# A decoder block on one core: the opening in fixed orders, four PSUM tiles for its transposes, and the first chunk's output in another slot

## The chip, the cores and the metric

The kernel runs on one core of one Trainium2 chip. The metric is the time on the device in microseconds, from the first to the last instruction and what lies around them; less is better.

## The reference

One layer of a hybrid block over 1024 positions of 1024 channels, in fp32:

```
h = LN(x)
xs, z, B, C, dt, glu, cgate = split(h @ w_in)            # 1024 x 5648
xs, B, C = silu(conv4([xs, B, C]))
y = ssd_chunked(xs, softplus(dt + b), -exp(a_log), B, C) + D * xs   # 8 chunks of 128
y_ssm = group_rms(y * silu(z)) * g
u = glu_a * sigmoid(glu_b);  u = silu(LN(conv31(u)));  y_conf = u * silu(cgate)
h = LN(alpha * h + [y_ssm, y_conf] @ w_out + b_out)
h = LN(alpha * h + sigmoid(h @ w_gate) * (p @ w_ple))
```

## The kernel before

**Products.** Each operand of a large product is split into an upper part rounded to fp32r and a rest (names with H and L, `woh`/`wol`, `wh`/`wl`), and `three` issues three matmuls per k-tile: upper by rest, rest by upper, upper by upper. ScalarE casts the upper part, VectorE or GpSimd (POOL) subtracts it for the rest (`split`).

**Stages.** (1) *Opening*: `ple_all` multiplies p by w_ple (tiles `wp`, `pp`; PSUM `psp`; result `pl` to DRAM); `embed` normalises x (8 tiles `xt` of 128 rows), transposes it by TensorE into PSUM tiles `pst`, applies gain and bias on ScalarE into an SBUF tile `htmp`, and VectorE casts and subtracts `htmp` into `hH[k]`, `hL[k]`, for each half of 512 positions. (2) *Projection*: 44 column tiles of `win`, each 8 k-tiles by two halves into `ps`; the first two, T_GA and T_GB, are computed half by half inside the opening. `dt_path` computes the time steps (`psd`, `psl`), the next tile after it is T_B. The 31-tap convolution runs on VectorE, for two tiles on ScalarE and POOL. `z_tile` stores silu(z) in DRAM (`z_d<-zt`). (3) *Scan*: eight chunks; matmuls `yd`, `yo`, `sp`, `pr`; VectorE evacuates `yd` into `y` (`inside`), POOL multiplies it by z (`gated`). The convolution half of the output projection (`pso`, steps of the generator `conf_out` taken by `turn`) fills TensorE between them. (4) *Output*: `out_proj` (`pss`; four series of 12 matmuls per chunk, evacuated by VectorE into `r`), transposes `pt`, and `gate` (`psg`).

**Storage.** SBUF tiles come from pools by tag, each tag with a fixed number of slots; a tile waits until the former tile in its slot is no longer used. `area` gives slots "W", "E", "M" (first used by hH and hL), `work` small rings ("y" has 2, "gt" 4). In PSUM `bank` has 3 tiles, `obank` 2, `bbank` 1, `pair` one of two banks.

**What sets the order.** A scheduler decides the order on each engine from its own estimate. Only instructions marked by `keep_in_program_order` keep the order in which they are written: TensorE's while `pinned` is set (the scan), and a few of VectorE. DMAs are all issued by SP, in one queue.

Of the kernel before, what the change touches and what calls it, by code (L numbers as in the profile page):

```python
# [36 lines left out]
NORM_ACT = (5, 7)  # L37
L_POOL = ()
# [8 lines left out]
def tile_block(ctx: ExitStack, tc: tile.TileContext, x, pT, wple, win, wdt, wout, wgate, vec, rows, heads, out):  # L47
    nc = tc.nc
    pinned = []

    def on_pe(ins):

        if pinned:
            tc.keep_in_program_order(ins)

    def mm(*args, **kw):
        on_pe(nc.tensor.matmul(*args, **kw))  # L57

    def transpose(**kw):
        on_pe(nc.tensor.transpose(**kw))  # L60
# [59 lines left out]
    nc.gpsimd.tensor_tensor(out=fold, in0=ident[:, 0:HEADS], in1=ident[:, HEADS:2 * HEADS], op=ALU.add)  # L120
    nc.gpsimd.tensor_tensor(out=fold, in0=fold, in1=ident[:, 2 * HEADS:3 * HEADS], op=ALU.add)
# [16 lines left out]
    def small(name, n):  # L138
        return wk.tile([P, n], F32, name=name, tag=name)

    def rstd_of(var, n, tag, eng):
        ve = small("ve" + tag, n)
        eng.tensor_scalar(out=ve, in0=var, scalar1=EPS, scalar2=None, op0=ALU.add)  # L143
        rs = small("rs" + tag, n)
        nc.gpsimd.tensor_tensor(out=rs, in0=ve, in1=mhalf[:, 0:n], op=ALU.pow)
        return rs

    def moments(src, tag):

# [16 lines left out]
    def embed_load(half):  # L166
        for t in range(half * 4, half * 4 + 4):
            nc.sync.dma_start(out=xts[t], in_=x[t * P:(t + 1) * P, :])

    def embed(half):  # L170
        for t in range(half * 4, half * 4 + 4):
            mu, rs = moments(xts[t], "0")
            if t in NORM_ACT:
                nm = small("nm0", 1)
                nc.gpsimd.tensor_scalar(out=nm, in0=mu, scalar1=rs, scalar2=-1.0, op0=ALU.mult, op1=ALU.mult)
                nc.scalar.activation(out=xts[t], in_=xts[t], func=AF.Identity, scale=rs, bias=nm)
            else:
                nc.vector.tensor_scalar(out=xts[t], in0=xts[t], scalar1=mu, scalar2=rs, op0=ALU.subtract, op1=ALU.mult)
        for k in range(NK):
            ps = obank("pst")  # L180
            for i in range(4):
                transpose(out=ps[:, i * P:(i + 1) * P], in_=xts[half * 4 + i][:, k * P:(k + 1) * P], identity=ident)
            if k % 2 == 0:
                both = work("htmp", "ha" if k == 4 else "gt")
            tmp = both[:, k % 2 * 512:k % 2 * 512 + 512]
            nc.scalar.activation(out=tmp, in_=ps, func=AF.Identity, scale=v("lng", k), bias=v("lnb", k))
            hs = slice(half * 512, half * 512 + 512)
            nc.vector.tensor_copy(out=hH[k][:, hs].bitcast(F32R), in_=tmp)  # L188
            leng = nc.gpsimd if k in L_POOL else nc.vector
            leng.tensor_tensor(out=hL[k][:, hs].bitcast(F32R), in0=tmp, in1=hH[k][:, hs], op=ALU.subtract)  # L190


    def weights(ct):
        raw, wh, wl = (regB.tile([P, NK, P], F32, name=n, tag="B2") for n in ("wraw", "wh", "wl"))
        nc.sync.dma_start(out=raw, in_=win[ct])
        split(raw, wh, wl, nc.gpsimd)
        return wh.bitcast(F32R), wl.bitcast(F32R)

    def inproj(ct, evac, halves=(0, 1), w=None):
        wh, wl = w or weights(ct)  # L200
# [10 lines left out]
    def residual():  # L211
        ag, abb, bob = (work(n, "ha") for n in ("ag", "abb", "bob"))
        for i, tl in enumerate((ag, abb, bob)):
            nc.sync.dma_start(out=tl, in_=rows[i:i + 1, :].broadcast_to([P, D]))
        nc.gpsimd.tensor_scalar(out=ag, in0=ag, scalar1=ALPHA, scalar2=0.0, op0=ALU.mult, op1=ALU.add)
        nc.gpsimd.tensor_scalar(out=abb, in0=abb, scalar1=ALPHA, scalar2=0.0, op0=ALU.mult, op1=ALU.add)
        nc.gpsimd.tensor_tensor(out=abb, in0=abb, in1=bob, op=ALU.add)

        for t in range(NT):
            nc.gpsimd.tensor_tensor(out=xts[t], in0=xts[t], in1=ag, op=ALU.mult)  # L220
            nc.gpsimd.tensor_tensor(out=xts[t], in0=xts[t], in1=abb, op=ALU.add)
            nc.sync.dma_start(out=ha_d[t], in_=xts[t])

    def ple_all():

        parts = {}
        tags = iter(["u", "u", "xd", "xd", "gt", "gt", "ha", "ha"])
        for src, nm in ((wple, "wp"), (pT, "pp")):
            for k in range(2):
                raw = work(nm + "raw", "xb") if nm == "wp" else regB.tile([P, L], F32, name=nm + "raw", tag="B2")  # L230
                parts[nm, k] = (raw, work(nm + "H", next(tags)), work(nm + "L", next(tags)))
        for half in range(2):
            hs = slice(half * 512, half * 512 + 512)
            for k in range(2):
                for src, nm in ((wple, "wp"), (pT, "pp")):
                    nc.sync.dma_start(out=parts[nm, k][0][:, hs], in_=src[:, k, hs])
                    split(*(a[:, hs] for a in parts[nm, k]), nc.vector)
        embed_load(0)
        nc.sync.dma_start(out=vc, in_=vec)
        nc.vector.tensor_scalar(out=hb, in0=v("bglu", 0, 16), scalar1=0.5, scalar2=None, op0=ALU.mult)  # L240
        parts = {i: (a[1].bitcast(F32R), a[2].bitcast(F32R)) for i, a in parts.items()}
        for t in range(NT):
            tk = slice(t * P, (t + 1) * P)
            pl = work("pl", "xb" if t % 4 > 1 else "y", L)
            for n in range(2):
                nn = slice(n * 512, n * 512 + 512)
                ps = bank("psp")
                for k in range(2):
                    three(ps, parts["pp", k][0][:, tk], parts["pp", k][1][:, tk], parts["wp", k][0][:, nn], parts["wp", k][1][:, nn], k == 0, k == 1)
                if (t + n) % 2:  # L250
                    nc.vector.tensor_copy(out=pl[:, nn], in_=ps)
                else:
                    nc.scalar.copy(out=pl[:, nn], in_=ps)
            nc.sync.dma_start(out=ple_d[t], in_=pl)

    def first_tap(act, o, src, w, b):
        if act:
            nc.scalar.activation(out=o, in_=src, func=AF.Identity, scale=w, bias=b)  # L258
        else:
            nc.vector.tensor_scalar(out=o, in0=src, scalar1=w, scalar2=b, op0=ALU.mult, op1=ALU.add)  # L260
# [4 lines left out]
    def conf_tile(j):  # L265
# [543 lines left out]
```

## Time and profile before

| | |
|---|---|
| median of 3 runs | 895.61 us (894.19 to 896.59) |
| the profiled execution | 894.83 us |
| its span, first to last instruction | 893.1 us |
| TensorE (PE) busy | 863.2 us, 97% |
| VectorE (DVE) | 641.2 us, 72% |
| POOL | 515.3 us, 58% |
| ScalarE (ACT) | 389.1 us, 44% |
| mean granted clock of TensorE | 0.99 |

The busy shares are means over four stages. Opening, first chunk and output have their own limits, and are read from windows and timelines. In a timeline a row is a start, a duration, and in brackets the idle time of the engine before it and who ended it; a matmul's duration is longer than its distance to the next, since matmuls overlap.

### The profile page before, as it was taken

The numbers are of one execution on the slowest core, as the hardware profiler recorded it, in microseconds if no ns is written. First come the engines' busy times: TensorE is split into PE (matmuls) and PEld (weight loads), VectorE is DVE, ScalarE is ACT, GpSimd is POOL, SyncE is SP. The second block draws the span as 40 slices with busy tenths as digits, with TensorE's granted clock in tenths as the row PEclk, the third lists the DMA queues.
The fourth block names the chain that finished last, engine by engine and source line by source line (L and its number), as shares of the span: only waits on it lengthen the run. The fifth ranks groups of instructions, "written<-read, shape, count | busy, mean of one in ns | idle before, by whom it ended". The sixth has DMA issues, their size and how long they took to land. (4 is left out here: it accounts for less than half of the span.)

```text
span 893.1 us, 10971 instructions
## 1 busy us (share of the span) xinstructions
PE 863.2 (97%) x4141; PEld 706.9 (79%) x4141; DVE 641.2 (72%) x739; ACT 389.1 (44%) x633; POOL 515.3 (58%) x297
## 2 busy tenths in 40 slices
PE   6989999999999999999999997999999799999996
PEld 4867888888888888888788885888888678888885
DVE  6968993799999989894403941676654796777765
ACT  4632336767333457553475735745453321111110
POOL 2559829999823299999572254766775362222111
PEclk9999999999999999999999998999999899999999
DMA  9702423121322314233241678799868812222212
GB/s 338 275 36 96 172 87 117 32 95 47 95 67 76 95 47 150 86 95 94 71 141 48 181 245 273 265 345 294 262 222 295 310 42 95 95 94 77 83 51 74
DMA packets 67716, 126.42 MB, mean 142 GB/s; under 512 B 4176, under 2 KB 41552, under 8 KB 67664
## 3 DMA queue, kind: packets, MB, share of 16 engines
q1 hardware_dynamic: 67664, 125.73, 42.1%
q8 instruction: 32, 0.52, 0.2%
q14 instruction: 20, 0.16, 0.1%
HBM read 89.93 MB, written 35.78 MB: 141 GB/s over the span
## 5 line engine op out<-in xcount | busy, mean ns | idle before, releaser
L57 PE MATMUL ps<-hL,wh 128*128 128x512 f32 x704 | 274.6, 391 | 1.1 <-DVE hL L190 1.1
L57 PE MATMUL ps<-hH,wl 128*128 128x512 f32 x704 | 274.2, 391 | 1.5 <-DVE hH L188 1.5
L57 PE MATMUL ps<-hH,wh 128*128 128x512 f32 x704 | 274.3, 390 | 0.0
L302 DVE SCALAR_TENSOR_TENSOR pc<-u,vc,pc 128x1024 f32<-128x1024 f32 x174 | 223.9, 1287 | 3.5
L297 POOL TENSOR_TENSOR acc<-acc,prod 128x1024 f32<-128x1024 f32 x60 | 146.4, 2440 | 17.9 <-ACT acc L293 15.0
L131 POOL TENSOR_TENSOR wl<-wraw,wh 128x1024 fp32r<-128x1024 f32 x44 | 110.7, 2515 | 77.1 <-PE ps L57 41.4
L57 PEld LDWEIGHTS ps<-hL,wh 128*128 128x128 f32 x704 | 132.2, 188 | 29.0 <-DVE hL L190 1.5
L57 PEld LDWEIGHTS ps<-hH,wl 128*128 128x128 f32 x704 | 131.8, 188 | 28.8 <-DVE hH L188 2.0
L57 PEld LDWEIGHTS ps<-hH,wh 128*128 128x128 f32 x704 | 132.2, 188 | 27.5 <-issue 0.2
L143 POOL TENSOR_SCALAR ve<-mv 128x1 f32<-128x1 f32 x23 | 15.8, 688 | 142.3 <-DVE mv L154 100.0
L296 ACT ACTIVATE prod<-u,vc 128x1024 f32<-128x1024 f32 x60 | 69.0, 1153 | 45.7 <-POOL acc L297 35.6
L130 ACT CAST wh<-wraw 128x1024 fp32r<-128x1024 f32 x44 | 46.2, 1051 | 67.0 <-DMA wraw<-in_win_dram 40.7
L643 ACT ACTIVATE gt<-psg 128x512 f32<-128x512 f32 (+1 forms) x17 | 9.7, 573 | 120.4 <-PE psg L57 120.4
L391 DVE SCALAR_TENSOR_TENSOR pc<-xin,vc,pc 128x512 f32<-128x512 f32 x72 | 53.7, 750 | 6.0 <-ACT pc L258 3.4
L57 PE MATMUL pss<-woh,yraw 128*128 128x512 f32 x128 | 51.3, 402 | 5.7 <-DVE r L616 5.7
L57 PE MATMUL pso<-woh,mL 128*128 128x512 f32 x128 | 53.6, 419 | 0.0
L57 PE MATMUL psg<-woh,hTL 128*128 128x512 f32 (+1 forms) x136 | 52.0, 383 | 0.0
L57 PE MATMUL psg<-woh,hTH 128*128 128x512 f32 (+1 forms) x136 | 52.0, 382 | 0.0
L616 DVE SCALAR_TENSOR_TENSOR r<-pss,rsm,r 128x512 f32<-128x512 f32 x32 | 23.8, 747 | 39.2 <-PE pss L57 32.7
L57 PE MATMUL psg<-wol,hTH 128*128 128x512 f32 (+1 forms) x136 | 51.5, 378 | 0.0
L57 PE MATMUL pss<-woh,yH 128*128 128x512 f32 x128 | 50.6, 396 | 0.0
L57 PE MATMUL pso<-wol,mH 128*128 128x512 f32 x128 | 50.6, 395 | 0.0
(184 smaller groups left out, 1460.7 us busy)
## 6 DMA issues: line engine op xcount, KB each, us to landing
wraw<-in_win_dram SPq DMA_DIRECT2D x44, 512.0 KB, 3.6
gt<-acs_d SPq DMA_DIRECT2D x16, 512.0 KB, 4.6
wor<-in_wout_dram SPq DMA_DIRECT2D x16, 512.0 KB, 5.6
xbc_d<-cacc SPq DMA_DIRECT2D x12, 512.0 KB, 3.4
xb<-xbc_d SPq DMA_DIRECT2D x8, 768.0 KB, 6.6
xt<-in_x_dram SPq DMA_DIRECT2D x8, 512.0 KB, 9.0
ple_d<-pl SPq DMA_DIRECT2D x8, 512.0 KB, 4.8
ha_d<-xt SPq DMA_DIRECT2D x8, 512.0 KB, 4.8
```

What stands on the lines that cost most here:

```text
L57: on_pe(nc.tensor.matmul(*args, **kw))
L130: nc.scalar.copy(out=h.bitcast(F32R), in_=src)
L131: leng.tensor_tensor(out=l.bitcast(F32R), in0=src, in1=h, op=ALU.subtract)
L143: eng.tensor_scalar(out=ve, in0=var, scalar1=EPS, scalar2=None, op0=ALU.add)
L296: nc.scalar.activation(out=pr, in_=u[:, i:i + L], func=AF.Copy, scale=v("ccw", j * KC + i))
L297: nc.gpsimd.tensor_tensor(out=acc, in0=acc, in1=pr, op=ALU.add)
L302: nc.vector.scalar_tensor_tensor(out=pc if i + 1 < KC else acc, in0=u[:, i:i + L], scalar=v("ccw", j * KC + i), in1=pc, op0=ALU.mult, op1= ...
L391: nc.vector.scalar_tensor_tensor(out=pc, in0=xin[:, o + j:o + j + 512], scalar=v("scw", i * 4 + j), in1=pc, op0=ALU.mult, op1=ALU.add)
L616: nc.vector.scalar_tensor_tensor(out=r[:, nn], in0=ps, scalar=rss[c][:, g:g + 1], in1=r[:, nn], op0=ALU.mult, op1=ALU.add)
L643: nc.scalar.activation(out=gt[:, nn], in_=ps, func=AF.Sigmoid)
```

## The change

**1. Opening.** `ple_all` and `embed` give way to `opening`, whose instructions keep their written order on all five queues. TensorE begins with 18 matmuls of `ones` by `ones` that nobody reads. The ple loads come in four pieces; four of eight ple steps stand ahead of the transposes, one between the halves, one inside the second half, two behind it. `pst` rotates over four PSUM tiles. The affine part is written in place, in PSUM, `htmp` is gone, and the casts and differences read PSUM. ScalarE normalises tiles 0, 1, 4, 5, 6 (before: 5, 7). T_B's weights and the time step's weights are prepared inside; the products `psd`/`psl` come after it.

**2. First chunk.** `y` of chunk 0 takes a slot of area "W"; the z loads of chunks 0 and 1 move behind `prep_load(2)`.

**3. Output.** The load of the second y chunk is issued behind all `wout` weights, its split goes from VectorE to POOL; the gate weights' splits and ScalarE's `woh` keep their written order.

```diff
+    def embed_turn(half, k):
+        ps = (obank, obank, bbank, pair)[k % 4]("pst")[:, 0:512]
+        for i in range(4):
+            transpose(out=ps[:, i * P:(i + 1) * P], in_=xts[half * 4 + i][:, k * P:(k + 1) * P], identity=ident)
+        turns[half, k] = ps
+    def embed_split(half, k, scalar):
+        ps = turns.pop((half, k))
+        hs = slice(half * 512, half * 512 + 512)
+        act.activation(out=ps, in_=ps, func=AF.Identity, scale=v("lng", k), bias=v("lnb", k))
+        if scalar:
+            act.copy(out=hH[k][:, hs].bitcast(F32R), in_=ps)
+        else:
+            dve.tensor_copy(out=hH[k][:, hs].bitcast(F32R), in_=ps)
+        dve.tensor_tensor(out=hL[k][:, hs].bitcast(F32R), in0=ps, in1=hH[k][:, hs], op=ALU.subtract)
...
+    def dummies(n):
+        warm = bbank("warm")
+        for _ in range(n):
+            mm(warm[:, 0:P], lhsT=ones, rhs=ones, start=True, stop=True)
...
+    def opening(eva, evb):
+        woven.append(True)
+        dummies(18)
...
+        ple_load("pp", 0, early)
+        ple_load("wp", 0)
+        ple_load("pp", 0, late)
+        ple_load("wp", 1)
+        embed_load(0, 2)
...
+        for k in range(4):
+            embed_turn(0, k)
...
+        turned_next = {0: (4,), 1: (5,), 2: (6,), 3: (7,)}
+        for k in range(NK):
+            embed_split(0, k, k not in (1, 2))
+            if k == 3:
+                ple_split("pp", 1, pool)
+
+            one(0, k, 0)
+            if k == 1:
+                one(0, 0, 1)
+            if k:
+                one(0, k, 1)
+            for i in turned_next.get(k, ()):
+                embed_turn(0, i)
+            if k in (4, 5):
+                embed_stats(k, True)
...
-    szs = [z_load(0)]
     eas.append(state_decay(1))
-    szs.append(z_load(1))
+    szs = []
...
-        y = slabs(work("y", "y"))
+        y = slabs(work("y", "y") if c else area("y", "W"))
...
             loaded = prep_load(c + 2)
+            if c == 0:
+                szs.extend((z_load(0), z_load(1)))
...
-        if k in (4, 6):
-            ys.append(y_load(len(ys)))
+        if k == 4:
+            ys.append(y_load(0))
...
+    ys.append(y_load(1))
...
-            wg = [out_weight(wgate[k], *regs[k], "xb" if k % 4 == 3 else None, leng=nc.vector if k % 2 else nc.gpsimd) for k in range(NK)]
+            wg = [out_weight(wgate[k], *regs[k], "xb" if k % 4 == 3 else None, leng=dve if k % 2 else pool, placed=True) for k in range(NK)]
```

ScalarE in the opening, before, from the first affine part to the evacuations of the first half of T_GA and T_GB (`ga`, `tb`):

```order
L186 ACTIVATE htmp<-pst,vc 128x512 x2
L176 ACTIVATE xt<-xt,nm_535,rs_533 128x1024
L253 COPY pl<-psp 128x512
L186 ACTIVATE htmp<-pst,vc 128x512
L130 CAST wh<-wraw 128x1024
L186 ACTIVATE htmp<-pst,vc 128x512
L253 COPY pl<-psp 128x512
L186 ACTIVATE htmp<-pst,vc 128x512 x2
L176 ACTIVATE xt<-xt,nm_557,rs_555 128x1024
```

And the same place of the kernel after, where every row has the line of one wrapper, L58:

```order
L58 CAST wh<-wraw 128x1024 x2
L58 ACTIVATE pst<-pst,vc 128x512
L58 CAST hH_125<-pst 128x512
L58 ACTIVATE pst<-pst,vc 128x512 x3
L58 CAST hH_128<-pst 128x512
L58 CAST ppH<-ppraw 128x512 x2
L58 ACTIVATE pst<-pst,vc 128x512
L58 CAST hH_129<-pst 128x512
L58 ACTIVATE pst<-pst,vc 128x512
```

The affine parts now alternate with casts of `hH` that VectorE did before, the `pl` copies and the normalised tiles stand elsewhere, and both weight casts stand ahead.

VectorE at the start of the output, before: `wol` are the rests of the output weights 4, 5, 3, 6, 7 in the order of the rows, `ha` evacuates the last `pso`, `r` the first `pss`:

```order
L131 TENSOR_TENSOR yraw<-yraw,yH 128x1024
L439 SCALAR_TENSOR_TENSOR wol<-wor,vc,woh 128x1024
L585 TENSOR_TENSOR ha<-ha,pso 128x512
L564 TENSOR_SCALAR vem<-pr 128x2
L439 SCALAR_TENSOR_TENSOR wol<-wor,vc,woh 128x1024
L585 TENSOR_TENSOR ha<-ha,pso 128x512
L439 SCALAR_TENSOR_TENSOR wol<-wor,vc,woh 128x1024
L131 TENSOR_TENSOR yraw<-yraw,yH 128x1024
L439 SCALAR_TENSOR_TENSOR wol<-wor,vc,woh 128x1024 x2
L616 SCALAR_TENSOR_TENSOR r<-pss,rsm_4430,r 128x512 x3
```

And after, with `wol` of the weights 4, 5, 6, 7, 3:

```order
L58 TENSOR_TENSOR yraw<-yraw,yH 128x1024
L58 SCALAR_TENSOR_TENSOR wol<-wor,vc,woh 128x1024
L58 TENSOR_TENSOR ha<-ha,pso 128x512
L58 TENSOR_SCALAR vem<-pr 128x2
L58 SCALAR_TENSOR_TENSOR wol<-wor,vc,woh 128x1024 x3
L58 TENSOR_TENSOR ha<-ha,pso 128x512
L58 SCALAR_TENSOR_TENSOR wol<-wor,vc,woh 128x1024
L58 SCALAR_TENSOR_TENSOR r<-pss,rsm_4444,r 128x512 x3
```

The second `yraw` has left VectorE, and the weight that stood third of five is the last ahead of `r`.

SP in the output, before, from the load of gate weights 2 to 5 to the load of the fourth y chunk:

```order
L433 DMA wor<-in_wgate_dram 128x1024 x4
L608 DMA r<-ha_d_82 128x1024
L433 DMA wor<-in_wgate_dram 128x1024
L592 DMA yraw<-y_d_90 128x1024
L433 DMA wor<-in_wgate_dram 128x1024
L592 DMA yraw<-y_d_91 128x1024
```

And after:

```order
L58 DMA wor<-in_wgate_dram 128x1024
L58 DMA r<-ha_d_82 128x1024
L58 DMA yraw<-y_d_90 128x1024
L58 DMA wor<-in_wgate_dram 128x1024 x2
L58 DMA yraw<-y_d_91 128x1024
L58 DMA wor<-in_wgate_dram 128x1024 x2
```

Of the eight gate weights one stood behind the load of the third y chunk before, and none behind the fourth; now two stand behind the third and two more behind the fourth.

## Rows read from the trace of the kernel before

**Rows 1.** Waits of TensorE: us in total, times, longest.

```profile
PE psp L57 <- DVE ppL L131: 6.1, 1, 6.1
PE pss L57 <- DVE r L616: 5.7, 2, 5.5
PE sp L57 <- DVE y L531: 5.0, 1, 5.0
...
PE ps L57 <- DVE hH L188: 1.5, 2, 0.9
```

**Rows 2.** Windows: length, busy PE, PEld, DVE, ACT, POOL, clock, DMA share, GB/s.

```profile
50.00:60.00 10.00, 7.44 (x35) 4.91 (x36) 9.93 (x9) 3.38 (x5) 7.42 (x4) 1.00 0.01 2
...
550.00:560.00 10.00, 6.85 (x18) 4.82 (x19) 3.45 (x10) 6.96 (x19) 2.82 (x2) 0.66 1.02 392
...
700.00:710.00 10.00, 5.81 (x17) 4.63 (x18) 5.55 (x6) 2.27 (x3) 2.39 (x1) 0.66 0.93 381
```

**Rows 3.** Timeline of TensorE: the opening, T_B's first matmul, and an fp32 product.

```profile
9.58 1.22 PE L57 MATMUL psp<-wpH,ppL 128*128 128x512 f32 x2 [1.83 <-ACT wpH L130]
...
14.87 0.63 PE L57 MATMUL psp<-wpH,ppL 128*128 128x512 f32 x1
...
15.68 0.39 PE L57 MATMUL psp<-wpH,ppH 128*128 128x512 f32 x1
...
18.45 0.40 PE L57 MATMUL psp<-wpH,ppH 128*128 128x512 f32 x1
...
76.06 0.40 PE L57 MATMUL ps<-hH,wl 128*128 128x512 f32 x1
...
153.46 0.39 PE L57 MATMUL psa<-dec,tri 128*128 128x128 f32 x2
153.69 0.39 PE L57 MATMUL psa<-dec,ones 128*128 128x128 f32 x2
```

**Rows 4.** Timeline of VectorE: `hL` from SBUF, and `r` from PSUM.

```profile
51.23 2.77 DVE L190 TENSOR_TENSOR hL<-htmp,hH 128x512 fp32r<-128x512 f32 x1
...
59.27 0.69 DVE L190 TENSOR_TENSOR hL<-htmp,hH 128x512 fp32r<-128x512 f32 x1
...
723.25 0.74 DVE L616 SCALAR_TENSOR_TENSOR r<-pss,rsm,r 128x512 f32<-128x512 f32 x1
```

**Rows 5.** Timeline of POOL at the same two times.

```profile
46.20 10.02 POOL L220 TENSOR_TENSOR xt<-xt,ag 128x1024 f32<-128x1024 f32 x4
...
722.21 3.38 POOL L131 TENSOR_TENSOR wol<-wor,woh 128x1024 fp32r<-128x1024 f32 x1
```

**Rows 6.** Groups of ScalarE, 0 to 30 us: busy, mean ns, idle before.

```profile
L130 ACT CAST wpH<-wpraw 128x512 fp32r<-128x512 f32 x4 | 2.5, 617 | 3.9 <-DMA wpraw<-in_wple_dram 3.8
L186 ACT ACTIVATE htmp<-pst,vc 128x512 f32<-128x512 f32 x2 | 1.5, 778 | 2.4 <-PE pst L60 2.4
```

**Rows 7.** Groups of VectorE, 0 to 30 us.

```profile
L152 DVE BATCH_NORM_STATS2 st<-xt 128x6 f32<-128x512 f32 x16 | 10.0, 669 | 0.0
...
L131 DVE TENSOR_TENSOR wpL<-wpraw,wpH 128x512 fp32r<-128x512 f32 x4 | 2.8, 692 | 6.4 <-ACT wpH L130 6.4
```

**Rows 8.** Timeline of VectorE in the first chunk.

```profile
551.88 2.15 DVE L531 SCALAR_TENSOR_TENSOR y<-xb,vc,yd 128x128 f32<-128x128 f32 x8 [15.84 <-DMA z_d<-zt]
```

**Rows 9.** Waits of all engines, whole span: ScalarE on the scan's loads.

```profile
ACT gt L464 <- DMA gt<-acs_d: 19.4, 3, 8.5
```

**Rows 10.** Timeline of TensorE in the output.

```profile
704.19 0.80 PE L57 MATMUL pss<-woh,yraw 128*128 128x512 f32 x1 [5.48 <-DVE r L616]
```

**Rows 11.** Timeline of VectorE in the output.

```profile
691.89 1.28 DVE L439 SCALAR_TENSOR_TENSOR wol<-wor,vc,woh 128x1024 fp32r<-128x1024 f32 x1
...
693.89 1.28 DVE L439 SCALAR_TENSOR_TENSOR wol<-wor,vc,woh 128x1024 fp32r<-128x1024 f32 x1
...
703.39 1.40 DVE L616 SCALAR_TENSOR_TENSOR r<-pss,rsm,r 128x512 f32<-128x512 f32 x2
```

**Rows 12.** Timeline of SP's DMA issues.

```profile
723.48 0.33 SPq L592 DMA_DIRECT2D yraw<-y_d  x1
```

More of the change, by code (lines that the diff above doesn't have):

```diff
@@ L164, in tile_block @@
     xts = [regB.tile([P, D], F32, name="xt", tag="B1") for t in range(NT)]
[L166 to L190, printed above, removed]
@@ L193, in weights, with embed_load, embed_stats @@
-    def weights(ct):
-        raw, wh, wl = (regB.tile([P, NK, P], F32, name=n, tag="B2") for n in ("wraw", "wh", "wl"))
-        nc.sync.dma_start(out=raw, in_=win[ct])
-        split(raw, wh, wl, nc.gpsimd)
+    def embed_load(t0, t1):
+        for t in range(t0, t1):
+            sync.dma_start(out=xts[t], in_=x[t * P:(t + 1) * P, :])
+    stats = {}
+    def embed_stats(t, scalar=False):
+        mu, rs = moments(xts[t], "0")
+        if scalar:
+            nm = small("nm0", 1)
+            pool.tensor_scalar(out=nm, in0=mu, scalar1=rs, scalar2=-1.0, op0=ALU.mult, op1=ALU.mult)
+            mu = nm
+        stats[t] = scalar, mu, rs
@@ L197, in weights @@
+    def weights(ct, loaded=None):
+        raw, wh, wl = loaded or weights_load(ct)
+        split(raw, wh, wl, pool)
         return wh.bitcast(F32R), wl.bitcast(F32R)
+    given = {}
     def inproj(ct, evac, halves=(0, 1), w=None):
-        wh, wl = w or weights(ct)
+        wh, wl = w or given.pop(ct, None) or weights(ct)
         for half in halves:
@@ L213, in residual @@
         for i, tl in enumerate((ag, abb, bob)):
[L214 to L217, printed above, removed]
+            sync.dma_start(out=tl, in_=rows[i:i + 1, :].broadcast_to([P, D]))
+        for a in (ag, abb):
+            tc.keep_in_program_order(pool.tensor_scalar(out=a, in0=a, scalar1=ALPHA, scalar2=0.0, op0=ALU.mult, op1=ALU.add))
@@ L219, in residual @@
+        pool.tensor_tensor(out=abb, in0=abb, in1=bob, op=ALU.add)
         for t in range(NT):
[L220 to L232, printed above, removed]
-            hs = slice(half * 512, half * 512 + 512)
[L234 to L244, printed above, removed]
-            for n in range(2):
[L246 to L260, printed above, removed]
+            pool.tensor_tensor(out=xts[t], in0=xts[t], in1=ag, op=ALU.mult)
+            pool.tensor_tensor(out=xts[t], in0=xts[t], in1=abb, op=ALU.add)
+            sync.dma_start(out=ha_d[t], in_=xts[t])
+    parts = {}
+    def ple_tiles(nm, half):
+        raw = slabs(work("wpraw", "xb", L) if nm == "wp" else regB.tile([P, L], F32, name="ppraw", tag="B2"), 2)
+        tags = {("wp", 0): "u", ("pp", 0): "xd", ("wp", 1): "gt", ("pp", 1): "ha"}
+        parts[nm, half] = raw, *(slabs(work(nm + i, tags[nm, half], L), 2) for i in "HL")
@@ new lines, in ple_load, with ple_split, ple_step, copy @@
+    def ple_load(nm, half, at=slice(0, 512)):
+        src = {"wp": wple, "pp": pT}[nm]
+        sync.dma_start(out=parts[nm, half][0][:, :, at], in_=src[:, :, half * 512 + at.start:half * 512 + at.stop])
+    def ple_split(nm, half, leng, at=None):
+        for i in [(slice(0, P), slice(0, 2), at)] if at else [(slice(0, P), k) for k in range(2)]:
+            split(*(a[i] for a in parts[nm, half]), leng)
+    pls = {}
+    def ple_step(t, n):
+        if n == 0:
+            pls[t] = work("pl", "xb" if t % 4 > 1 else "y", L)
+        ps = bank("psp")
+        nn = slice(n * 512, n * 512 + 512)
+        tk = slice(t % 4 * P, t % 4 * P + P)
+        for k in range(2):
+            w, p = ([a[:, k, :].bitcast(F32R) for a in i[1:]] for i in (parts["wp", n], parts["pp", t // 4]))
+            three(ps, p[0][:, tk], p[1][:, tk], w[0], w[1], k == 0, k == 1)
+        def copy():
+            act.copy(out=pls[t][:, nn], in_=ps)
+            if n:
+                sync.dma_start(out=ple_d[t], in_=pls[t])
+        return copy
@@ L449, in heads3, with behind @@
         return a.rearrange("p (h d) -> p h d", d=HD)
+    def behind(here, ins):
+        if here:
+            tc.keep_in_program_order(ins)
     def prep_load(c):
         xb = slabs(work("xb", "xb", 12 * P), 12)
-        nc.sync.dma_start(out=xb, in_=xbc_d[c])
+        sync.dma_start(out=xb, in_=xbc_d[c])
         gg = []
```

382 lines of the change are left out of this document (241 added, 141 removed).

## The prediction

> **What bounds the kernel now.** I read the page's first part, then TensorE's list of waits, then the windows in which its busy time is short, then the timelines of those places. By the page TensorE is busy for 863.2 of 893.1 us, so at most 29.9 us of its idle time can go, and 8 us of that is the tail behind the last matmul. The list says where the rest lies [rows 1]: 6.1 us before the first matmul, 5.7 in the output projection behind VectorE's `r`, 5.0 in the first chunk of the scan behind VectorE's `y`, and small ones in the opening. The windows show the same holes [rows 2]: 2.56 us of ten between 50 and 60, 3.15 between 550 and 560, 4.19 between 700 and 710.
>
> They also show a second loss. In the last two windows the granted clock is 0.66, so 6.8 of the ten microseconds stood at half rate; part of that lies in the wait itself, part in work behind it. In the opening the clock column reads 1.00, but the starts tell it: from 9.58 to 14.87 the matmuls of 128x512 follow each other at 0.44 us (twelve steps), from 15.68 to 18.45 at 0.23 (twelve steps) [rows 3]. The rate rose after some 5.7 us of work without a gap. So everything before about 15.3 ran at the lower level.
>
> From 76.06, the first matmul of tile T_B, to the scan, and between the two late holes, TensorE has no wait worth naming. What is won at the ends of such stretches stays won as long as the other engines have slack; the page gives them 72% at most.
>
> **The change part by part.**
>
> *The opening.* Up to T_B TensorE has 96 `psp`, 96 `ps` and 32 `psd`/`psl` matmuls, 224 x 0.23 = 51.5 us [rows 3], and 64 transposes; an fp32 matmul of 128x128 is two records, and the next one starts 0.23 later [rows 3], so a record costs 0.115, and the transposes, one record each, 7.4. With 1 us for the small transposes of the time steps (an estimate by the same row) it is 60 us of work at full rate. It reaches T_B at 76.06: 16 us are lost, of which the start takes 6.1, the gap behind it 1.8 [rows 3], the half rate 3.5 (17 matmuls x 0.21), and the holes between 50 and 60, on hH in the first place, 2.6 [rows 1, 2].
>
> The 18 added dummies are fp32 128x128, two records each: 0.23 us at full rate, 0.43 at half, 4.1 to 7.7 us together. They need only `ones`, so they can run from about 1.3 us (an estimate: TensorE waits for nothing but POOL's fill). Rising 5.7 us later, as before, the clock is up at about 7 and they end near 8. The data is no earlier than that: the loads are the same bytes in four pieces, and the second weight slab, which ended the gap at 9.58, comes a little sooner. So `psp` starts at 8.2 (7.1 to 9.2) at full rate, against the 11.4 lost before: 3.2 us won.
>
> Then 48 `psp` end at 19.2. The first transposes need the fourth normalised x tile. VectorE gets there after eight splits of 0.69, eight BN_STATS of 0.67 [rows 7] and about 3 us of small work, from a first load at 4 to 5 us and two load waits: near 19.6. TensorE waits, and its 16 transposes end at 21.5. In the first half ScalarE has eight affines of 0.78, six casts and two `ppH` casts of 0.62 [rows 6], some 11.2 us, behind two weight casts that end near 22, and a step of VectorE and six matmuls behind the last: 37, where TensorE alone, with 14.7 us of work, would be done at 36. So this half gives back 3 us in thin stretches. The second half has the copies spread (four casts on VectorE), and TensorE needs 1.8 us a step against 1.1 for ScalarE and 0.9 for VectorE: no wait there, and the 2.6 us of holes between 50 and 60 go. 8.2 + 60 + 3 gives T_B at 71.2: 4.9 us won. Bounds: 1 (ScalarE's fixed queue holds up both halves, and the clock falls once in the thin stretch at 20 to 26, 3.4 us) to 7 (nothing is given back).
>
> The new operands lie in PSUM. Before, hL from SBUF took 0.69 us alone and 2.77 while POOL ran its four products [rows 4, 5]; `r<-pss`, with a PSUM operand, took 0.74 at 723.25 while POOL was at work [rows 4, 5]. So I take 0.69 for hL and 0.42 to 0.62 for the casts from PSUM. The Trainium skill, "VectorE: DVE Perf Modes", section "Two Vector instructions with no wait between them", says that the second SBUF read interface is shared with GpSimd and is read by an operation with two SBUF inputs; hL now has one. The trace agrees (0.74 against 2.77). Without that rule the sum would be the slower rival's below.
>
> What is moved behind the opening (dt products, residual products, `ple` steps) lands where VectorE and POOL have slack; I cost it at nothing. If the cover were gone, a POOL product of 2.5 us [rows 5] would be the unit of the loss.
>
> *The first chunk.* `y` of chunk 0 moves to a slot that the last projection tile frees, so VectorE no longer waits for the z write; it sat 15.84 us before `y`, to 551.88 [rows 8]. The 5.0 us of TensorE go, and the half-rate work behind: TensorE is busy 6.85 us in that window, of which I take 5.2 at half rate, 2.6 saved (bounds 0 and 3.4). 7.6 together. What is late next: the z loads still wait for the z write, so the gate product of chunk 0, its Square and the mean-square matmul of chunk 1 are no earlier; and the DMA share is 1.02 there [rows 2], where ScalarE waits for the `gt` loads of the next chunks, 8.5 us at the longest [rows 9]. Starting 7.6 us sooner, TensorE catches up with these. I give back 2 us for the one and 1.6 for the other: 4.0 net (0 to 8).
>
> *The output.* In the wait of 5.48 us before 704.19 [rows 10] TensorE wants `r` to free the PSUM bank; VectorE does `r` at 703.39, behind the split of yraw(1) and two `wol` that ran beside POOL [rows 11]. Now yraw(1) goes to POOL, and the three `wol` come together. That wait (5.5) and its half-rate part (2.1) go: 7.6. But `wol` of weight 3, done at 693.89 before [rows 11], is now last: from 691.89 three `wol` of 1.28, one `ha` of 0.69 and itself, 691.89 + 4 x 1.28 + 0.69 = 697.7. The eleventh `pss` of a series that starts at 693.1 needs it at 695.4: 2.3 us lost. And the last two gate weights are now loaded behind yraw(3), which SP issued at 723.48 [rows 12] when the second projection had freed its slot; some 5 us sooner that is 718, plus 4 to 5.6 for the load, 1 for the cast and 2.4 to 3.4 for POOL: 726 to 728, where the seventh gate weight is wanted at about 726. I take 0.9 (0 to 3). Net 7.6 - 2.3 - 0.9 = 4.4 (2 to 7.5).
>
> *Sum.* 4.9 + 4.0 + 4.4 = 13.3. The profiled execution took 894.83 (span 893.1 and 1.7 around it), 0.8 under the median 895.61; less 13.3 it is 881.5, and the median 882.3. I say 882.
>
> **The rivals.**
>
> *The scan gives its part back (A).* Chunk 0 starts earlier, but the loads set the pace of chunks 2 to 4: shares of 0.92 to 1.02 [rows 2] and ScalarE's waits for `gt` [rows 9] speak for it; against it, that TensorE had no listed wait in those chunks before, so there is some slack. Gain 9.3: 886.
>
> *The opening gives its part back (B).* Eight fixed steps across three in-order queues, with one affine, one or two copies and six matmuls each, leave short waits all over and the clock down again. For it: ScalarE is the fuller queue, and it dropped to half rate in every hole of 5 us [rows 2]. Against: holes of about 1 us between 50 and 60 left the clock at 1.00 [rows 2]. Gain 8.4: 887. The Trainium skill, "TensorE: Matmul & The Clock Gate", section "HAM oscillation — how this bites in real kernels", says that groups of matmuls with waits between them can run at the lower clock again and again; these rows show it only for the long waits.
>
> *Everything hides (C).* Opening 7, scan 7, output 6: 875.5.
>
> *Slower (D).* VectorE's copies from PSUM are slowed by POOL after all, as those from SBUF were: hL 2.77 for 0.69 [rows 4]. Then a step of half one costs 2.1 us more for the four k that run beside POOL's weight splits (8 us), and each step of half two takes 3.4 for VectorE instead of 1.8 for TensorE (8 x 1.6 = 13). The opening then loses 16 where it won 4.9, and the rest (8.4) does not pay for it: 902. It decides from about 2 us per hL on; then opening and rest cancel. The row of `r<-pss` [rows 4] and POOL's order, with little of its heavy work in half two, speak against it.
>
> That nothing changes is not to be had: the slot of `y` is different, and with it the wait.
>
> **How the numbers follow.** Forecast 882, itself 878 to 885: 0.52. A 0.15, B 0.14, C 0.10, D 0.05; 0.04 for losses of A, B and the output together, about 894. Two in ten left out gives 875 to 891 (opening 1, scan 1 and output 2.5 make 891). A measurement here tells 0.3%, 2.7 us, from no change. Faster 0.90, within it 0.04, slower 0.06.
>
> **What would show it.** Right: TensorE's waits on `y` and on `r` are gone and the clock of the two windows is 1.00; the first `psp` is at about 8.2 at 0.23 spacing; T_B starts near 71; a new wait of about 2 us on `wol` stands in the first `pss` series. Wrong: hL in the opening over 1 us; T_B at 75 or later; new waits of TensorE in chunks 1 to 3 of over 4 us together, or on `psg` of over 3.

## The result, and the profile after

| | before | after |
|---|---|---|
| median | 895.97 us (894.19 to 896.59, 4 runs) | 882.39 us (881.94 to 883.46, 4 runs) |
| profiled execution, span | 894.83, 893.1 | 883.46, 881.7 |

The ratio is 0.9853, 95% interval 0.9836 to 0.9871: 13.6 us faster by the medians, 11.4 in the two profiled executions. Of after, the slowest of the four runs was profiled.

TensorE's waits of after (columns as in [rows 1]):

```profile
PE pr L58 <- POOL ea L58: 2.8, 1, 2.8
PE ps L58 <- POOL wl L58: 2.3, 1, 2.3
...
PE pss L58 <- DVE ha L58: 1.0, 1, 1.0
PE pss L58 <- DVE r L58: 0.4, 1, 0.4
```

The waits of `psp`, `sp` and `hH` of [rows 1] are gone, and that on `r` is 0.4. Two new ones of 2.8 and 2.3 stand first. (`pr` is the mean square of the chunk before, which POOL's `ea` feeds; `xtok`, in later lists, is the transposes of a chunk's loaded inputs `xb`; `warm` is the dummies.) TensorE's windows of after, for [rows 2] and the two that hold the new waits (length, busy time, clock, DMA share, GB/s):

```profile
20.00:30.00 10.00, 7.68 (x37) 0.83 1.01 335
50.00:60.00 10.00, 10.00 (x49) 1.00 0.23 84
550.00:560.00 10.00, 10.00 (x82) 1.00 1.06 322
560.00:570.00 10.00, 7.20 (x25) 0.85 0.92 313
700.00:710.00 10.00, 10.00 (x50) 1.00 0.62 215
```

The three short windows of [rows 2] are now filled at clock 1.00, and two others are short, at 0.83 and 0.85. Timeline of TensorE in the opening, for [rows 3]:

```profile
1.18 7.16 PE L58 MATMUL warm<-ones 128*128 128x128 f32 x36 [1.18 <-POOL ones L58]
8.10 0.48 PE L58 MATMUL psp<-wpH,ppL 128*128 128x512 f32 x1
...
19.18 0.40 PE L58 MATMUL psp<-wpH,ppH 128*128 128x512 f32 x1
19.42 1.91 PE L58 MATMUL pst<-ident,xt 128*128 128x128 f32 x16
...
23.63 0.49 PE L58 MATMUL ps<-hH,wl 128*128 128x512 f32 x1 [2.31 <-POOL wl L58]
...
26.75 0.63 PE L58 MATMUL ps<-hH,wh 128*128 128x512 f32 x1
27.18 0.63 PE L58 MATMUL ps<-hH,wl 128*128 128x512 f32 x1
...
72.38 0.50 PE L58 MATMUL ps<-hH,wl 128*128 128x512 f32 x1
```

The dummies end at 8.1, the 48 `psp` run to 19.4 at full rate, and T_B starts at 72.38 for 76.06. Between them is a hole of 2.3 us, and behind it some 3.5 us of matmuls at 0.43, the half rate.

This hole is not the same in every execution. Kernel after was profiled once more (experiment 8); there the dummies end sooner, the hole is 1.05 us, the clock of the window stays at 1.00, and T_B starts at 70.07. Three rows of that execution:

```profile
1.18 6.10 PE L58 MATMUL warm<-ones 128*128 128x128 f32 x36 [1.18 <-POOL ones L58]
22.66 0.50 PE L58 MATMUL ps<-hH,wl 128*128 128x512 f32 x1 [1.05 <-POOL wl L58]
```

```profile
20.00:30.00 10.00, 8.95 (x49) 1.00 1.00 349
```

Six profiled executions have exactly this opening: the two of after, and one each of experiments 1, 2, 3 (the opening alone) and 7. In them the hole before the first `ps` is 0.73 to 2.31 us, T_B starts at 70.07 to 72.69 (71.3 on average), and the first scan matmul `yd` at 537.91 to 540.50 (539.1 on average). The first profile of after lies at the late end of all three.

Three marks split the profiled spans: the first `yd` of the scan, the first `pss`, and the last matmul.

| | first `yd` | scan, to `pss` | output, to the last matmul |
|---|---|---|---|
| before | 543.69 | 149.40 | 191.70 |
| after | 540.24 | 147.66 | 185.59 |
| won | 3.4 | 1.7 | 6.1 |
| after, second profile | 537.91 | 148.91 | 185.13 |
| won | 5.8 | 0.5 | 6.6 |

### The profile page after: what moved, and what is told of

Read it like the earlier page. It is cut to its first block, busy times and chain, and to the rows that moved or that the text cites. A ratio compares the mean times of both kernels' runs of the same rounds, so it can differ in the third digit from the quotient of the medians.

```text
span 881.7 us, 11049 instructions
## 1 busy us (share of the span) xinstructions
PE 865.0 (98%) x4177; PEld 710.9 (81%) x4177; DVE 623.1 (71%) x731; ACT 401.5 (46%) x654; POOL 511.2 (58%) x287
## 4 chain that ended last, share of the span: by engine, by line
PE 88%; DMA 5%; DVE 2%; issue 1%; POOL 1%; ACT 1%; SPq 0%; DVEq 0%; POOLq 0%; ACTq 0%
PE ps L58 55%; PE psg L58 10%; PE pss L58 10%; PE pso L58 5%; DMA xb<-xbc_d 2%; PE psp L58 1%; PE yd L58 1%; DMA ea<-ea_d 1%; DMA wor<-in_wout_dram 1%; DVE y L58 1%; PE yo L58 1%; PE pt L58 1%; PE sp L58 1%; DMA gt<-acs_d 1%; DMA wpraw<-in_wple_dram 1%
## 5 line engine op out<-in xcount | busy, mean ns | idle before, releaser
L58 PE MATMUL ps<-hH,wl 128*128 128x512 f32 x704 | 276.5, 393 | 2.3 <-POOL wl L58 2.3
L58 PE MATMUL ps<-hL,wh 128*128 128x512 f32 x704 | 274.8, 390 | 0.0
L58 PE MATMUL ps<-hH,wh 128*128 128x512 f32 x704 | 274.8, 390 | 0.0
L58 DVE SCALAR_TENSOR_TENSOR pc<-u,vc,pc 128x1024 f32<-128x1024 f32 x174 | 223.8, 1286 | 3.7
L58 PEld LDWEIGHTS ps<-hH,wl 128*128 128x128 f32 x704 | 132.5, 188 | 29.9 <-POOL wl L58 2.5
L58 PEld LDWEIGHTS ps<-hL,wh 128*128 128x128 f32 x704 | 132.5, 188 | 27.7 <-DVE hL L58 0.3
L58 PEld LDWEIGHTS ps<-hH,wh 128*128 128x128 f32 x704 | 132.4, 188 | 27.6
L58 POOL TENSOR_TENSOR acc<-acc,prod 128x1024 f32<-128x1024 f32 x60 | 145.2, 2421 | 16.2 <-ACT acc L58 13.1
L58 POOL TENSOR_TENSOR wl<-wraw,wh 128x1024 fp32r<-128x1024 f32 x44 | 108.5, 2466 | 79.0 <-PE ps L58 41.6
L58 ACT ACTIVATE prod<-u,vc 128x1024 f32<-128x1024 f32 x60 | 68.9, 1153 | 54.5 <-POOL acc L58 34.8
L58 POOL TENSOR_TENSOR rs<-ve,mhalf 128x1 f32<-128x1 f32 x24 | 21.9, 913 | 104.0 <-DVE ve L58 96.3
L58 ACT CAST wh<-wraw 128x1024 fp32r<-128x1024 f32 x44 | 46.0, 1049 | 59.6 <-DMA wraw<-in_win_dram 33.8
L58 ACT ACTIVATE gt<-psg 128x512 f32<-128x512 f32 (+1 forms) x17 | 9.7, 573 | 114.3 <-PE psg L58 114.3
L58 DVE SCALAR_TENSOR_TENSOR pc<-xin,vc,pc 128x512 f32<-128x512 f32 x72 | 53.6, 748 | 7.6 <-ACT pc L58 7.1
L58 PE MATMUL pso<-woh,mL 128*128 128x512 f32 x128 | 53.2, 416 | 0.0
L58 PE MATMUL pss<-woh,yraw 128*128 128x512 f32 x128 | 50.8, 397 | 1.4 <-DVE ha L58 1.0
L58 PE MATMUL psg<-woh,hTH 128*128 128x512 f32 (+1 forms) x136 | 51.9, 381 | 0.0
L58 PE MATMUL psg<-woh,hTL 128*128 128x512 f32 (+1 forms) x136 | 51.8, 383 | 0.0
L58 PE MATMUL psg<-wol,hTH 128*128 128x512 f32 (+1 forms) x136 | 51.5, 378 | 0.0
L58 PE MATMUL pso<-wol,mH 128*128 128x512 f32 x128 | 50.7, 396 | 0.0
L58 PE MATMUL pso<-woh,mH 128*128 128x512 f32 x128 | 50.5, 394 | 0.0
L58 PE MATMUL pss<-woh,yH 128*128 128x512 f32 x128 | 50.0, 390 | 0.0
```

The source lines that it names most:

```text
L58: ins = method(*args, **kw)
```

## The experiments

Three parts were undone, alone and together; then each new wait was attacked. All kernels were timed in turn with the kernel before, and a time is read against the 895.3, 894.9 or 895.8 us that before took in the same session.

**1. The first chunk undone.**

```diff
-        y = slabs(work("y", "y") if c else area("y", "W"))
+        y = slabs(work("y", "y"))
```

with the z loads ahead again, and the chunk-2 loads free.

> The kernel after with the first chunk's part undone: y of chunk 0 in the ring that the last z tile holds, the z loads of chunks 0 and 1 ahead, the chunk-2 loads free again. Read from one trace of each kernel, the part is worth little: TensorE reached its first scan matmul 3.45 us earlier than before and the first matmul of the output 5.19 earlier, so 1.7 us were won between. Theory A (the scan gave most of the 7.6 us back through the new 2.8 us wait of pr on POOL, the half-rate stretch behind it and the 1.1 us wait of xtok on its load): about 884.1, 1.7 over the kernel after. Rival (the prediction's term): 4.0 more, 886.4. Rival (nothing given back): 7.6 more, 890. In all of them the wait of sp on y must be back, about 5 us, with a window at clock 0.66.

884.03 us, ratio 0.9879 (0.9866 to 0.9892): 2.3 us of the gain go by the ratios, give or take 2 by the two intervals. Waits of TensorE, and two windows (columns as above):

```profile
PE sp L58 <- DVE y L58: 3.2, 1, 3.2
```

```profile
540.00:550.00 10.00, 6.77 (x46) 0.87 1.08 319
550.00:560.00 10.00, 10.00 (x52) 0.79 0.96 375
```

The wait on `y` and the fall of the clock are back, though shorter and milder than the expected 5 us and 0.66, and the wait of `pr` is gone. The part took away one hole and opened another, as theory A has it. The time alone does not exclude the rival's 4.0; the traces speak for theory A, since the scan takes 148.50 us here and 147.66 and 148.91 in the two profiles of after.

**2. The output undone.**

```diff
-        if k == 4:
-            ys.append(y_load(0))
+        if k in (4, 6):
+            ys.append(y_load(len(ys)))
...
-        split(raw, yH, raw, pool if c else dve, c == 1)
+        split(raw, yH, raw, dve if c < 2 else pool)
```

with the gate weights' splits and ScalarE's output weights free again.

> The kernel after with the output part undone: second y chunk loaded between the output weights and split on VectorE, gate weights' splits and ScalarE's output weights free again. Theory (the traces of before and after: output stage to the end took 200.0 us before and 193.8 after): 6.2 more, 888.6, with the wait of pss on r of about 5.5 us and a window at clock 0.66 back. Rival (the prediction's term): 4.4 more, 886.8.

890.47 us, ratio 0.9954 (0.9938 to 0.997): 9.0 us of the gain go, more than either theory said. TensorE waits, and the window behind:

```profile
PE pss L58 <- DVE r L58: 6.5, 2, 6.2
```

```profile
690.00:700.00 10.00, 3.78 (x16) 0.91 0.89 350
700.00:710.00 10.00, 10.00 (x35) 0.75 0.54 204
```

The output takes 193.70 us here, 194.16 in the opening alone of experiment 3, and 191.70 in the one trace of before. Whether that trace was a mild case of the wait on `r`, or the new opening makes the old output worse, is not shown.

**3. Opening alone, and the two others alone.** The first is the kernel after with the edits of 1 and 2, the second the kernel before with the change's edits of these two parts.

> The kernel after with both the first chunk's and the output's parts undone, so the opening alone against the kernel before. Theory (in the traces the opening brings the first scan matmul 3.4 us earlier, and nothing behind it changes): 895.3 - 3.4 = 891.9. Rival (the parts are not additive: without the opening the two others gained only 6.5 of the 13, so the opening is worth 6 whatever stands behind it): 889.3. Rival (waits on y and r swallow it): above 894.

> The kernel before with the first chunk's and the output's parts of the change, and without the new opening (its order, dummies and PSUM tiles). The two undone parts cost 1.6 and 8.1 us against the kernel after. Theory (the parts add up): 895.3 - 1.6 - 8.1 = 885.6, so the opening is worth 3.2 to 3.8. Rival (the opening's 3.5 us are the larger share because the output gains only 6.2 as the two traces have it): 887.5. Rival (the output's fixed order fits only the shifted schedule): above 889.

The opening alone: 890.99 us, ratio 0.9947 (0.993 to 0.9965), 4.8 us won. Without it: 888.48, ratio 0.9909 (0.988 to 0.9939), 8.1 by the ratio, 6.5 by the medians. Together 11.3 to 12.9 of 13.6: the parts nearly add up, with nothing to choose between the first two theories within the intervals. Undone one at a time, the two others look larger: 2.3 and 9.0 (experiments 1 and 2), which with the opening's 4.8 make 16.1. With the output undone, undoing the first chunk as well costs nothing more (890.99 against 890.47). So the worth of the first chunk's part depends on the others, or is lost in the noise. Waits of the opening alone, and of the kernel without it:

```profile
PE pss L58 <- DVE r L58: 7.6, 2, 7.4
PE sp L58 <- DVE y L58: 4.7, 1, 4.7
```

```profile
PE pr L57 <- POOL ea L561: 2.8, 1, 2.8
```

The waits on `y` and `r` come with the old parts, whatever the opening, and that of `pr` with the new first chunk. The profile of the opening alone is that of the slowest of its ten runs (895.32 us, the fastest 887.94).

**4. No dummies.**

```diff
-        dummies(18)
```

> The kernel after without the 18 dummies; nothing else in the order changes. The first psp starts where it did, near 8.2, but at half rate until the clock rises, some 5.7 us later, so the 48 psp end about 2.6 us later, near 22. Theory 1 (dummies are worth their full 2.6 us): 885.0. Theory 2 (the weight rest wl on POOL is ready at 23.6 in any case, and is what the first ps waited for): nearly all of it is hidden, T_B is reached 0 to 0.7 us later, and since the hole of 2.3 us is filled the clock doesn't fall at 23.6, which gives back up to 2.0: 880.9 to 883.

884.02 us, ratio 0.989 (0.9875 to 0.9905): 1.6 by the medians, 3.3 by the ratio (of after 0.9853). Theory 1's 2.6 lies between the two; theory 2 allowed 0.6 at most. Timeline of TensorE:

```profile
7.45 0.80 PE L58 MATMUL psp<-wpH,ppL 128*128 128x512 f32 x1 [7.45 <-ACT wpH L58]
...
10.90 0.43 PE L58 MATMUL psp<-wpL,ppH 128*128 128x512 f32 x1
11.16 0.39 PE L58 MATMUL psp<-wpH,ppH 128*128 128x512 f32 x1
...
24.48 0.71 PE L58 MATMUL ps<-hH,wl 128*128 128x512 f32 x1 [2.30 <-POOL wl L58]
```

The products start 0.65 us sooner than in the first profile of after, and the half rate lasts 3.5 us, not 5.7. T_GA's first matmul comes 0.85 us later, and the hole before it is as long as there. In this pair it hides nothing, since ScalarE's copies, and with them `wl`, move along. The last of the 48 `psp` starts at 20.04, against 18.19 to 19.49 (19.0 on average) in the six executions with dummies.

**5. The weights earlier.** Casts of both weights pulled ahead, the last ple copy behind the first affine part:

```diff
         ple_step(1, 1)()
+        w = [weights(None, lo[0])]
...
         ple_step(2, 1)()
+        w.append(weights(None, lo[1]))
```

> The kernel after with the casts of T_GA's and T_GB's weights pulled ahead on ScalarE, behind the second and third ple copies of the second half, and the last ple copy put behind the first affine part; POOL's wl follow. Theory (the hole of 2.3 us before the first ps and the half rate to 27.6 behind it come from wl alone): the hole shrinks to 0.5 at most, the clock stays up, T_B is reached 3 to 4 us earlier, 878.4 to 879.4. Rival (ScalarE's affine chain is the bound of the first half, and wl only the last to come): 0.5 to 1.5 us, 881 to 882.

879.68 us, ratio 0.9839 (0.9819 to 0.9858), 1.3 us below after by the ratios and within the intervals. The first `yd` came at 539.75, only 0.5 earlier than in the first profile of after and later than the average without the edit. TensorE, VectorE and POOL:

```profile
22.02 2.88 PE L58 MATMUL pst<-ident,xt 128*128 128x128 f32 x13 [2.55 <-DVE xt L58]
```

```profile
19.14 2.83 DVE L58 TENSOR_SCALAR xt<-xt,mv,rs 128x1024 f32<-128x1024 f32 x1 [0.44 <-POOL rs L58]
21.89 2.32 DVE L58 TENSOR_SCALAR hb<-vc 128x16 f32<-128x16 f32 x1
```

```profile
19.08 5.10 POOL L58 TENSOR_TENSOR wl<-wraw,wh 128x1024 fp32r<-128x1024 f32 x2
```

`wl` now starts 0.06 us before the last normalisation on VectorE, from SBUF to SBUF, and that takes 2.83 us where the one before it took 0.80. The hole moved from the first `ps` to the transposes. The scan of this execution was 2.9 us shorter than after's, at a wait of `pr` of 2.6 us behind which the clock stayed up. The edit touches nothing there, so that share of the time is not put down to it.

**6. The weights behind the normalisation.** Both casts after the third ple copy of the second half.

> As f1_weights_early, but both weight casts behind the third ple copy of the second half, so that POOL starts wl near 19.6 and not at 18.4. In f1 the hole before the first ps was gone, but POOL's wl ran beside VectorE's normalisation of the fourth x tile, SBUF to SBUF, which took 2.83 us for 0.80, and the transposes waited 2.6 us for it. Theory (port contention moved the hole): here the normalisation takes 0.8 again, the holes before 24 us add to 1.0 or less, the clock stays up, and the first scan matmul comes 2.5 us earlier than in the kernel after, 537.7; time 878 to 880. Rival (the hole only moves again): the first scan matmul at 539.5 to 540.3.

880.04 us, ratio 0.9823 (0.9783 to 0.9862); first `yd` at 537.85, 2.4 us earlier than in the first profile of after. VectorE:

```profile
19.23 0.81 DVE L58 TENSOR_SCALAR xt<-xt,mv,rs 128x1024 f32<-128x1024 f32 x1 [0.44 <-POOL rs L58]
19.96 2.33 DVE L58 TENSOR_SCALAR hb<-vc 128x16 f32<-128x16 f32 x1
22.21 0.68 DVE L58 TENSOR_TENSOR hL<-pst,hH 128x512 fp32r<-128x512 f32 x1
```

The normalisation now begins 0.49 us before `wl` (19.72) and takes its usual 0.81, and the holes add up to 1.1 us. What begins beside `wl` now is `hb`, of 16 columns: 2.33 us. `hL` stood behind it and began 0.34 us after the cast that it needs was done (21.87); an earlier `hb` was not tried.

The theory's start of the scan, 537.7, is met, but that does not show what the edit is worth: after itself, in its second profile, reached the first `yd` at 537.91 without it. Three executions with the edit (this one and the two of experiment 8) have T_B at 69.88 to 70.21 and `yd` at 537.7 to 538.1; the six without it have 70.07 to 72.69 and 537.91 to 540.50. In these few executions the edit makes the good case regular, 1.2 us earlier on average. In the times this does not show: the intervals of this kernel and of after overlap.

Without dummies this kernel gave 882.09 us, ratio 0.9848 (0.9826 to 0.987), 2.0 to 2.2 more, with the first `yd` 1.2 later. That is near the theory, but the two intervals allow 4 us either way, so the rival is not excluded:

> f1c_weights_after_norm without the 18 dummies. In d1_no_dummies, where wl hid a part, they were worth 1.6 us and the first scan matmul came only 0.65 later. Theory (with the hole behind them mostly closed, the half-rate start shows: 12 to 13 psp at 0.2 us more, 2.5 us): 2 to 2.6 over f1c, 882 to 882.6, first scan matmul near 540. Rival (the transposes wait for VectorE's normalised tile in any case, at about 19.6): 0.5 to 1.2 over f1c, 880.5 to 881.2.

**7. The Square first.** ScalarE's Square of chunk 0, which feeds `pr` through POOL's `ea`, kept ahead of the decay products of chunk 2:

```diff
-        act.activation(out=sq, in_=y.rearrange("p (g t) l -> p g t l", g=2), func=AF.Square)
+        behind(c == 0, act.activation(out=sq, in_=y.rearrange("p (g t) l -> p g t l", g=2), func=AF.Square))
...
-            act.activation(out=xdd[:, h * HD:(h + 1) * HD], in_=xdt[:, h * HD:(h + 1) * HD], func=AF.Copy, scale=col(dec, c, h))
+            behind(c == 2, act.activation(out=xdd[:, h * HD:(h + 1) * HD], in_=xdt[:, h * HD:(h + 1) * HD], func=AF.Copy, scale=col(dec, c, h)))
```

The place in after, on ScalarE, POOL and TensorE:

```profile
556.90 3.94 ACT L58 ACTIVATE xdd<-xdt,dec 128x64 f32<-128x64 f32 x16
560.74 1.05 ACT L58 ACTIVATE ea<-y 128x1024 f32<-128x1024 f32 x1
```

```profile
554.30 2.39 POOL L58 TENSOR_TENSOR y<-y,sz 128x1024 f32<-128x1024 f32 x1 [0.89 <-DMA sz<-z_d]
...
565.66 0.72 POOL L58 TENSOR_TENSOR ea<-ea 128x256 f32<-128x256 f32 x1
```

```profile
566.44 0.61 PE L58 MATMUL pr<-inv,ea 128*128 128x1 f32 x4 [2.80 <-POOL ea L58]
566.91 0.67 PE L58 MATMUL pso<-woh,mL 128*128 128x512 f32 x1
567.38 0.63 PE L58 MATMUL pso<-wol,mH 128*128 128x512 f32 x1
```

`y` was ready at 556.7, the Square began at 560.74.

> The kernel after with ScalarE's Square of chunk 0 kept ahead of the 16 decay products of chunk 2, which it stood behind. Theory (the 2.8 us wait of pr on POOL's ea, and the half rate of 8 matmuls behind it, come from that order alone): the wait and the dip of the clock at 560 to 570 go, the scan is 2 to 4 us shorter, 878.5 to 880.5. Rival (the DMA share of 0.92 to 1.06 sets the pace of chunks 1 to 4, so the time returns as waits on loads): 881.5 to 882.5, with new waits of xtok, yd or sp.

878.2 us, ratio 0.9808 (0.9767 to 0.9849). TensorE's wait on the scan:

```profile
PE xtok L58 <- DMA xb<-xbc_d: 2.8, 2, 2.5
```

The time is 4.0 us below after by the ratios, and the intervals allow about as much either way. The wait of `pr` is gone, as the theory has it, so ScalarE's order was its cause; the next wait is on a load, as the rival has it.

**8. Both.**

> f1c and f2 together. Theory (they add up): the sum of both gains, 874.5 to 877.5. Rival (an earlier scan meets its loads earlier, so that the second gain is lost to the waits on DMA): the better of the two alone, 878 to 880.

878.55 us, ratio 0.9805 (0.9766 to 0.9844): no better than 7 alone, and in the range of the rival. Once more beside the kernel after:

> The kernel after once more, on one chip with the three others, as their measure: 882.4, 881 to 884.

> f12c_both on the same chip as the kernel after, for the distance of the two: 3.5 to 4.5 us below after_again. If the wait of xtok on xb, 2.6 us, is what is left of the scan's loss, it stands in this trace again, and the wait of pr on ea doesn't.

After 882.2 us, ratio 0.9848 (0.9828 to 0.9868); with both edits 877.61, ratio 0.9806 (0.9788 to 0.9823): 4.6 us below after by the medians and 3.8 by the ratios, whose intervals do not overlap. All five runs lie below all four of after. The wait of `pr` is gone, and the longest wait of TensorE is that of `xtok` on its load `xb`, 2.0 us. In the second profile of after, of which rows stand above, `pr` waits 3.7 us and `xtok` not at all.

## Why the prediction was right or wrong

The time was right (882 forecast, 882.39 measured), and so are the three places from which it comes. Two of the three terms were mis-sized, in opposite directions, and nearly cancel: that part of the hit is luck.

| term | forecast | first profile | second profile | by undoing |
|---|---|---|---|---|
| opening | 4.9 | 3.4 | 5.8 | 4.8 (alone) |
| first chunk | 4.0 | 1.7 | 0.5 | 2.3 |
| output | 4.4 | 6.1 | 6.6 | 9.0 |

*The start of the opening: right in time, its cause in part.* 8.2 was forecast for the first `psp` at full rate; it came at 8.10, and at 7.04 in the second profile. The 3.2 us credited to the start are not the dummies' price. Without them (experiments 4 and 6) the last of the 48 `psp` starts at 20.04 and 20.27, with them at 19.0 on average: 1.0 to 1.3 us. The rest is there without them: in experiment 4 no gap of 1.83 us [rows 3] stands behind the first products, and the full rate is reached at 10.9 instead of 15.7. The times put the dummies at 1.6 to 3.3 and 2.0 to 2.2 us, with wide intervals. The step "rising 5.7 us later" did not hold as a constant either: in experiment 4 the rate rose 3.5 us after the first matmul.

*The first half of the opening: the size was right on average, its cause wrong.* 3 us of thin stretches were put down to ScalarE's affine chain. The six executions have instead one hole of 0.73 to 2.31 us on POOL's `wl`, which had been left out of the chain, some with up to 1.1 us more on the normalised tile, and in two of them, both with a hole of 2.31, some 3.5 us at half rate behind it. In after that is 2.3 + 1.7 = 4.0 us lost, in its second profile 2.0. T_B came at 71.3 on average, for 71.2, and the first `yd` 4.5 us before that of the old opening (543.6 and 543.7), for 4.9. The sum behind the forecast does not come out: 36 for TensorE alone counts the first 16 transposes twice (by its own numbers it is 34.4), and the parts named for ScalarE give 35.3, not 37.

*PSUM operands: right.* `hL` took 0.68 to 0.69 beside POOL's `wl`, where the SBUF operand took 2.77 [rows 4]. So the slower rival D fell. (Its 902 should read 903: 895.6 + 16 - 8.4.) VectorE's casts from PSUM took 0.69, more than the 0.42 to 0.62 taken; it had the slack.

*The first chunk: the mechanism right, the size wrong.* The waits on `y` and the half rate went. The term of 3.6 us given back was too small: by the two profiles 1.7 and 0.5 of 7.6 stayed, by experiment 1 2.3 (give or take 2), against 4.0 forecast. The wait of `pr` was foreseen at 2 us and took 2.80 and 3.71, and the 8 and 13 matmuls at half rate behind it, about 1.7 and 2.7 us, were not in the sum. Its cause was mainly ScalarE's order (experiment 7) and not the z load, for which POOL waited 0.89 us. So by the two profiles rival A came nearer in the scan than the forecast, though not for its reason: the wait on a load, `xtok`, is 1.1 us or none, and comes to the front only when `pr` is mended.

*The output: mis-sized the other way.* 7.6 less 2.3 less 0.9 was the sum. The 7.6 held in the profiled pair, and 6.1 of it stayed, against 4.4. The step that failed is that the eleventh `pss` needs `wol` of weight 3. TensorE of before, then TensorE and VectorE of after:

```profile
698.10 0.39 PE L57 MATMUL pss<-wol,yH 128*128 128x512 f32 x1
```

```profile
687.90 0.40 PE L58 MATMUL pss<-woh,yraw 128*128 128x512 f32 x1
...
689.97 0.39 PE L58 MATMUL pss<-woh,yraw 128*128 128x512 f32 x1
691.38 0.50 PE L58 MATMUL pss<-woh,yraw 128*128 128x512 f32 x1 [1.03 <-DVE ha L58]
...
694.28 0.39 PE L58 MATMUL pss<-wol,yH 128*128 128x512 f32 x1
```

```profile
689.45 1.28 DVE L58 SCALAR_TENSOR_TENSOR wol<-wor,vc,woh 128x1024 fp32r<-128x1024 f32 x1 [0.26 <-ACT woh L58]
690.65 0.68 DVE L58 TENSOR_TENSOR ha<-ha,pso 128x512 f32<-128x512 f32 x1
691.25 1.28 DVE L58 SCALAR_TENSOR_TENSOR wol<-wor,vc,woh 128x1024 fp32r<-128x1024 f32 x1
```

The eleventh in time, at 691.38, is the first of the second series, and it resumes as `ha` ends, with the last `wol` just begun: by the profile it waited for `ha`, which empties a PSUM tile and stood behind three `wol` in VectorE's fixed order. The first series' own eleventh and twelfth, which read weight 3, come behind the whole second series, at 694.28, and the second series reads that weight as its last, at 693.82, when its `wol` was done (692.53). The trace of before already had this order (698.10). The wait was 1.03 us, and 0.68 in the second profile, instead of 2.3, and the gate weights, whose last loads were issued at 712 and not 718, cost nothing. That the undone output costs 9.0 us (experiment 2), more than 7.6, stays open.

So the sum, 13.3, was met by 3.4 + 1.7 + 6.1 = 11.2 in the first profile, 5.8 + 0.5 + 6.6 = 12.9 in the second, and 13.6 in the medians; a part too high and one too low nearly cancel. Of the signs named, the waits on `y` and `r`, the clock of the two windows and, on average, T_B came out; the wait on `wol` did not, and `pr` and `xtok`, 3.9 us together, stayed just under the 4 that would have spoken against it.

## What to carry to other kernels

When a wait is taken away, ask of the next instruction in the fixed order of every engine, not only of the data that was late: here `pr`, `wl` and `ha` each waited because another engine did something less urgent first (experiment 7 shows it for `pr`; for `wl` and `ha` it is read from the order). Undo the parts one by one: a total that is right does not say that its terms are. Profile the same kernel twice before a mark that moved by 2 us is put down to an edit: here the mark moves as much by itself. And before weights are split earlier on POOL, look at what VectorE does from SBUF beside it.

## What was not expected of the hardware

Two VectorE operations with one SBUF source that began beside POOL's 2.4 us `wl` were not slowed in proportion: `hb`, 128x16, took 2.32 and 2.33 us in experiments 5 and 6, and 0.17 in after, where POOL was idle; the 128x1024 normalisation took 2.83 for 0.80. Both lose about 2 us, as if they waited for one POOL instruction to end: in experiment 6 the first `wl` ends at 22.26 and `hb` at 22.29. `hL`, with one operand in PSUM, took 0.68 all the same. Nor is every operation that reads SBUF held up: in before, two BN_STATS began and ended beside a `wl` of POOL at their usual 0.6 us each:

```profile
21.22 1.24 DVE L152 BATCH_NORM_STATS2 st<-xt 128x6 f32<-128x512 f32 x2
```

```profile
20.51 2.40 POOL L131 TENSOR_TENSOR wl<-wraw,wh 128x1024 fp32r<-128x1024 f32 x1 [3.27 <-ACT wh L130]
```

The same hole does not always cost the clock. A wait of `pr` of 2.80 us in after was followed by half rate, one of 2.92 in experiment 6 by a window at 0.67; one of 3.16 in experiment 6 without dummies left it at 1.00:

```profile
560.00:570.00 10.00, 7.08 (x19) 0.67 0.98 330
```

```profile
560.00:570.00 10.00, 6.84 (x29) 1.00 0.89 300
```

The first is experiment 6, the second the same without dummies. What decides it stays open. The runs of one kernel lie up to 7 us apart (the opening alone in experiment 3), and how much of that comes from the clock is not shown.
